# Where the tiles of a Trainium2 encoder kernel lie inside an SBUF partition

## The chip, the cores and the metric

The kernel runs on one core of one Trainium2 chip. The metric is the device time of one execution in microseconds (us), as the median over several runs. The kernel before takes 1402.52 us (three runs, 1402.32 to 1404.49).

## The reference, cut to what matters

One layer of a hybrid encoder block over a sequence of 256 positions with 2048 channels, all in float32. What is computed is almost wholly matrix products with large weights:

```
h = rms_norm(x, g_mix)
qa, ka, va, qb, kb, vb, qc, gates = split(h @ w_in)        # 2048 -> 4096 + 3 * 2048
oa, ob, oc = three attentions (mixer A dilated, B grouped-query, C over fixed memory tokens)
merged = sum over branches of sigmoid(gate_i) * (o_i @ w_br_i)
x = x + merged @ w_o                                        # 2048 -> 2048
hf = rms_norm(x, g_ffn) @ w_ffn_in                          # 2048 -> 2 * 5632
x = x + (silu(hf[:, :5632]) * hf[:, 5632:]) @ w_ffn_out     # 5632 -> 2048
```

## The kernel before

**Products.** The 256 positions are the output rows, in two tiles of 128. Weights come in blocks of 128 partitions by two times 512 columns of float32 (4096 bytes in each partition). Each block goes through three steps. SyncE's queue issues its load into a tile `raw` (line 202, `load`). ScalarE copies it, rounded, into a tile `whi`, and VectorE writes the remainder `raw - whi` into a tile `wlo` (lines 363 and 373, or 124 and 125): these are the two **halves** of a block. TensorE then makes three products of 128 by 128 by 512 for each piece: activations' high part with `whi`, high part with `wlo`, low part with `whi` (lines 225 to 227 in `product`, 402 to 404 in `pair`). The half of the weights is the moving operand, which streams 512 columns (2048 bytes of a partition) past the array; the activations (`memT`, `xT`, `oT`, `mT`, `x1T`, `hT` and the sums called `forms`) are the stationary operand, 128 columns (512 bytes) that a LDWEIGHTS brings in ahead of each matmul. In the profile a matmul is written as output<-moving,stationary, as in `mmZ<-whi,x1T`.

**Stages.** First the products of the memory tokens and of q, k and v, with the attentions beside them (`beginning`, then `product` at line 695); then four gate blocks and the branch A blocks (lines 701 to 709); then, in `everything()`, merging, the output projection, and the feed-forward layer. The stages of `everything()` use `pair`, which takes two blocks of weights at a time in a fixed order of steps (lines 53 to 58), some of them through a scheme of seven products in place of eight. `run` keeps TensorE four steps behind the halves (`run(everything(), 4)`, line 874). SyncE's queue and TensorE are held in the order of the program, and `follow` does the same for the halves on ScalarE and VectorE; the rest is placed by a scheduler.

**Pools.** All of these tiles lie in one SBUF partition's address range, at the same place in each of the 128 partitions. Pools are laid one behind another in the order in which they are opened, from low addresses up (`side="right"`: from the top down). Below them all lies a ring for DMA descriptors of 16,384 bytes. `wp` holds six `raw` tiles, four `whi` and four `wlo` of 4096 bytes each; `big` holds eleven tiles of 8192 bytes (`memT`, `xT`, `oT`, `x`, `x1T`, `mg`, most `forms`); `mid` five of 4096; `small` little ones. `early` (constants and loads of the start) and `s2` (sixteen tiles of 2048 bytes for heads of the attentions) are closed by `heads.close()` at line 711, and their room is given to two later pools: `tail` (four tiles of 8192 bytes: `mT`, `hT` and a few `forms`) and `more` (one further `whi` and one further `wlo`). `halves` (line 353) takes the tiles of `more` in every fifth call, and those of `wp` in the others:

```
356        pool, n = (more[0], 1) if more and count[0] % 5 == 0 else (wp, 4)
357        hi = pool.tile([P, PK, NC], F32R, name="whi", bufs=n)
358        lo = pool.tile([P, PK, NC], F32R, name="wlo", bufs=n)
```

Of the kernel before, what the change touches and what calls it, by code (L numbers as in the profile page):

```python
# [11 lines left out]
F32 = mybir.dt.float32  # L12
# [6 lines left out]
P = 128  # L19
# [6 lines left out]
NC = 512  # L26
KF = DFF // P
PK = 2
# [70 lines left out]
def encoder_block(ctx: ExitStack, tc: tile.TileContext, a: dict, out: bass.AP):  # L99
    nc = InOrder(tc)  # L100
    const = ctx.enter_context(tc.tile_pool(name="const", bufs=1))
    wp = ctx.enter_context(tc.tile_pool(name="wp", bufs=3))
    big = ctx.enter_context(tc.tile_pool(name="big", bufs=11))
    mid = ctx.enter_context(tc.tile_pool(name="mid", bufs=5))
    small = ctx.enter_context(tc.tile_pool(name="small", bufs=4))
    dram = ctx.enter_context(tc.tile_pool(name="dram", bufs=1, space=bass.MemoryType.DRAM))
    heads = ExitStack()
    early = heads.enter_context(tc.tile_pool(name="early", bufs=1))
    psum = ctx.enter_context(tc.tile_pool(name="psum", bufs=4, space=bass.MemoryType.PSUM))

    def s8(shape, name, dt=F32R, pool=None):
# [48 lines left out]
    side, now = [], [0]  # L160
# [33 lines left out]
    def finish():  # L194
        while side:
            tick()

    def load(src, k0, nk):

        raw = wp.tile([P, PK, NC], F32, name="raw", bufs=6)  # L200
        c = k0 % PK * NC
        nc.sync.dma_start(out=raw[:, :nk].rearrange("p k n -> p (k n)"), in_=src[k0 // PK][:, c:c + nk * NC])
        return raw

    def product(src, lhs, nk, head=(), beside={}):


        ps = [bank("mm", "mm") for _ in range(T)]
        k0 = 0
        while k0 < nk:  # L210
            n = head[0] if head else min(PK, nk - k0)
            head = head[1:]
            if k0 in beside:
                start(beside[k0])
            lhs(k0)
            raw = load(src, k0, n)
            hi = wp.tile([P, PK, NC], F32R, name="whi", bufs=4)
            lo = wp.tile([P, PK, NC], F32R, name="wlo", bufs=4)
            split(hi[:, :n], lo[:, :n], raw[:, :n])
            for i in range(n):  # L220
                k = k0 + i
                xh, xl = lhs(k)
                for t in range(T):
                    c = slice(t * P, (t + 1) * P)
                    nc.tensor.matmul(ps[t], lhsT=xh[:, c], rhs=hi[:, i], start=(k == 0), stop=False)
                    nc.tensor.matmul(ps[t], lhsT=xh[:, c], rhs=lo[:, i], start=False, stop=False)
                    nc.tensor.matmul(ps[t], lhsT=xl[:, c], rhs=hi[:, i], start=False, stop=(k == nk - 1))
                tick()
            k0 += n
        return ps  # L230
# [120 lines left out]
    count, more = [0], []  # L351
# [23 lines left out]
    def pair(src, lhs, order, done, forms=None, operand=None):  # L375
# [47 lines left out]
        def whole(u, c):  # L423
            def ready():
                if operand and c == 0:
                    operand(2 * u, True)
                raw = load((src(u, c),), 0, PK)
                if operand and c == 0:
                    if 2 * u + 2 < KT:
                        operand(2 * u + 2, True)  # L430
                    operand(2 * u)
                hi, lo = halves(raw)

                def products():
                    for k in range(2):
                        for t in range(T):
                            mul(("YV", "ZQ")[c][t], at(2 * u + k, t), hi[:, k], lo[:, k])
                return products
            return ready
# [3 lines left out]
        def first(u):  # L443
            def ready():
                b1, b2 = (load((src(u, c),), 0, PK) for c in range(2))
                held[u] = b1, b2
                hi, lo = halves(b1)

                def products():
                    mul("X", at(2 * u, 0), hi[:, 0], lo[:, 0])  # L450
                    mul("Y", at(2 * u + 1, 0), hi[:, 1], lo[:, 1])
                    if left["X"] == 2 * seven:
                        tl["A"], tl["B"] = s4([P, 2, NC], "SA"), s4([P, 2, NC], "SB")
                        copy(("A", 0), "X")
                return products
            return ready
# [252 lines left out]
            nc.vector.tensor_mul(mg[t][:, n0:n0 + NC], bp[t], sg[:, t])  # L709
    finish()  # L710
    heads.close()
    tail = ctx.enter_context(tc.tile_pool(name="tail", bufs=4))
    more.append(ctx.enter_context(tc.tile_pool(name="more", bufs=1)))
    mT, x1T, x = [], [], []
    ss1 = const.tile([P, T, 4], F32, name="ss1")

# [243 lines left out]
```

## Time and profile before

| | |
|---|---|
| median of three runs | 1402.52 us |
| profiled execution, its own time | 1403.52 us |
| its span | 1401.7 us, so 1.8 us lie around it |
| TensorE matmuls (PE) | 1384.8 us busy, 99% of the span, 6248 instructions |
| LDWEIGHTS (PEld) | 1137.0 us, 81% |
| VectorE (DVE) | 1118.3 us, 80% |
| ScalarE (ACT) | 807.7 us, 58% |
| granted TensorE clock, mean | 0.999 |
| HBM traffic | 197 GB/s over the span |

A busy PE in such a page is not a PE at its peak: matmuls overlap, and a matmul's recorded duration is longer than the distance to the next one's start. What a matmul costs in a full stream is the distance from start to start. The chain of waits shows that best: it merges successive matmuls of one output into pieces, each with its start, its length and the count (x3 is three matmuls).

### The profile page before, as it was taken

To read this page: it belongs to the slowest core of one execution; us is meant where nothing else is said; L and a number is where in the kernel's file an instruction comes from. 1 tells how busy PE (TensorE), PEld (TensorE's weight loads), DVE (VectorE), ACT (ScalarE), POOL (GpSimd) and SP (SyncE) were. 2 spreads that over 40 slices of the span, in tenths; PEclk is the share of its full clock that TensorE was granted. 3 is DMA by queue.
4 is the path that set the end of the run, shared out by engine and by line. 5 is a ranking of instruction groups with operands and counts; after the bars stand their busy time and mean duration, and the time that the engine had idled before them with its cause. 6 is when DMAs were issued, how large, how long until landed. Compare 5 with 4: busy or idle time off the path is not lost.

```text
span 1401.7 us, 17524 instructions
## 1 busy us (share of the span) xinstructions
PE 1384.8 (99%) x6248; PEld 1137.0 (81%) x6248; DVE 1118.3 (80%) x1474; ACT 807.7 (58%) x1093; POOL 76.7 (5%) x146
## 2 busy tenths in 40 slices
PE   8999999999999999999999999999999999999998
PEld 6778878888888888888888888888888888888887
DVE  5767756754798888788988997989988988988863
ACT  6766546544465564646665565655565665566632
POOL 0024533200000000000000000000000000000000
PEclk9999999999999999999999999999999999999999
DMA  8976535556565565755656665666655656565653
GB/s 300 336 238 212 164 103 189 161 161 192 173 232 201 182 213 179 272 177 182 195 168 207 210 184 192 195 210 195 214 189 183 222 179 203 191 198 191 222 167 125
DMA packets 79416, 277.09 MB, mean 198 GB/s; under 512 B 8992, under 2 KB 11552, under 8 KB 79072
## 3 DMA queue, kind: packets, MB, share of 16 engines
q1 hardware_dynamic: 79184, 275.94, 60.3%
q8 instruction: 49, 0.80, 0.2%
q14 instruction: 39, 0.32, 0.1%
q10 hardware_dynamic: 144, 0.02, 0.0%
HBM read 273.05 MB, written 2.88 MB: 197 GB/s over the span
## 4 chain that ended last, share of the span: by engine, by line
PE 92%; POOL 2%; DMA 2%; DVE 1%; ACT 1%; issue 1%; SPq 0%; DVEq 0%; ACTq 0%; POOLq 0%
PE mm L74 17%; PE mmZ L74 16%; PE mmV L74 16%; PE mmY L74 16%; PE mmQ L74 13%; PE mmX L74 9%; PE mmW L74 3%; DMA raw<-in_w_mem 2%; PE tp L74 1%; PE sc L74 1%; POOL rot L593 1%; DVE wlo L125 0%; POOL rot L590 0%; DMA rows<-in_mem 0%; PE o L74 0%
## 5 line engine op out<-in xcount | busy, mean ns | idle before, releaser
L363 ACT ACTIVATE whi<-raw 128x1024 fp32r<-128x1024 f32 (+1 forms) x454 | 451.5, 1004 | 343.2 <-PE mmQ L74 103.1
L373 DVE TENSOR_TENSOR wlo<-raw,whi 128x1024 fp32r<-128x1024 f32 (+1 forms) x454 | 517.9, 1154 | 106.9 <-ACT whi L363 104.6
L74 PE MATMUL mm<-whi,xT 128*128 128x512 f32 x768 | 244.0, 394 | 0.0
L125 DVE TENSOR_TENSOR wlo<-raw,whi 128x1024 fp32r<-128x1024 f32 x100 | 128.6, 1295 | 86.1 <-ACT whi L124 84.8
L74 PEld LDWEIGHTS mm<-whi,xT 128*128 128x128 f32 x768 | 144.0, 189 | 29.5 <-issue 0.8
L124 ACT ACTIVATE whi<-raw 128x1024 fp32r<-128x1024 f32 x100 | 105.6, 1070 | 89.9 <-PE mm L74 83.9
L74 PE MATMUL mm<-wlo,xT 128*128 128x512 f32 x384 | 150.8, 393 | 0.1
L74 PE MATMUL mmY<-whi,x1T 128*128 128x512 f32 x288 | 112.5, 392 | 0.0
L74 PE MATMUL mmV<-whi,x1T 128*128 128x512 f32 x288 | 109.7, 393 | 0.0
L373 DVE TENSOR_TENSOR wlo<-t,whi 128x1024 fp32r<-128x1024 f32 x74 | 72.5, 994 | 37.5 <-ACT whi L363 37.0
L363 ACT ACTIVATE whi<-t 128x1024 fp32r<-128x1024 f32 x74 | 63.0, 869 | 47.3 <-PE mmV L74 26.8
L74 PE MATMUL mmZ<-whi,x1T 128*128 128x512 f32 x224 | 87.5, 391 | 0.0
L74 PE MATMUL mmQ<-whi,x1T 128*128 128x512 f32 x224 | 87.4, 390 | 0.0
L74 PEld LDWEIGHTS mm<-wlo,xT 128*128 128x128 f32 x384 | 72.5, 189 | 15.7 <-issue 0.8
L74 PE MATMUL mmX<-whi,forms 128*128 128x512 f32 x232 | 78.9, 392 | 0.0
L74 PEld LDWEIGHTS mmY<-whi,x1T 128*128 128x128 f32 x288 | 54.0, 188 | 12.0
L74 PEld LDWEIGHTS mmV<-whi,x1T 128*128 128x128 f32 x288 | 54.0, 188 | 11.6
L74 PE MATMUL mmY<-whi,hT 128*128 128x512 f32 x156 | 60.6, 393 | 0.0
L74 PE MATMUL mmV<-whi,hT 128*128 128x512 f32 x156 | 60.2, 392 | 0.0
L74 PE MATMUL mmY<-wlo,x1T 128*128 128x512 f32 x144 | 56.3, 391 | 0.0
L74 PE MATMUL mmV<-wlo,x1T 128*128 128x512 f32 x144 | 56.3, 391 | 0.0
L74 PE MATMUL mmZ<-whi,hT 128*128 128x512 f32 x136 | 53.9, 396 | 0.0
(258 smaller groups left out, 2700.0 us busy)
## 6 DMA issues: line engine op xcount, KB each, us to landing
raw<-in_w_ffn SPq DMA_DIRECT2D x176, 512.0 KB, 4.3
raw<-in_w_gate SPq DMA_DIRECT2D x96, 512.0 KB, 4.2
raw<-in_w_ffn_out SPq DMA_DIRECT2D x88, 512.0 KB, 4.4
raw<-in_w_qkv SPq DMA_DIRECT2D x64, 512.0 KB, 4.5
raw<-in_w_o SPq DMA_DIRECT2D x32, 512.0 KB, 4.5
raw<-in_w_br SPq DMA_DIRECT2D x24, 512.0 KB, 4.3
raw<-in_w_mem SPq DMA_DIRECT2D x16, 512.0 KB, 5.7
rawT<-in_memT SPq DMA_DIRECT2D x8, 256.0 KB, 4.1
```

Source lines behind the costliest of these rows:

```text
L74: ins = op(*args, **kw)
L124: nc.scalar.activation(hi, src, AF.Copy)
L125: nc.vector.tensor_sub(lo, src, hi.bitcast(F32))
L363: nc.follow(nc.scalar.activation(hi[:, o], v, AF.Copy))
L373: nc.follow(nc.vector.tensor_sub(*due.pop(0)))
L593: op(ov[:, :, :, c], ov[:, :, :, c], tmp[:, :n])
```

## The change

Every instruction stays, and only the place of the tiles inside a partition is changed. `wp` now holds only the halves, behind `const` and `small` at the bottom of the partition, with a filler of 96 bytes (`fill`) that brings the first of them to byte 12288 = 3 x 4096. `raw` gets a pool of its own, `rp`, and `rp`, `big` and `mid` are laid from the top of the partition down. The ring for DMA descriptors shrinks to 8192 bytes. `more` is opened ahead of `tail`, so that it comes to lie right behind the four `wlo` of `wp`.

```
-    wp = ctx.enter_context(tc.tile_pool(name="wp", bufs=3))
-    big = ctx.enter_context(tc.tile_pool(name="big", bufs=11))
-    mid = ctx.enter_context(tc.tile_pool(name="mid", bufs=5))
     small = ctx.enter_context(tc.tile_pool(name="small", bufs=4))
+    wp = ctx.enter_context(tc.tile_pool(name="wp", bufs=4))
+    rp = ctx.enter_context(tc.tile_pool(name="rp", bufs=6, side="right"))
+    big = ctx.enter_context(tc.tile_pool(name="big", bufs=11, side="right"))
+    mid = ctx.enter_context(tc.tile_pool(name="mid", bufs=5, side="right"))
...
+    small.tile([P, 24], F32, name="fill", bufs=1)
...
-        raw = wp.tile([P, PK, NC], F32, name="raw", bufs=6)
+        raw = rp.tile([P, PK, NC], F32, name="raw")
...
     heads.close()
+    more.append(ctx.enter_context(tc.tile_pool(name="more", bufs=1)))
     tail = ctx.enter_context(tc.tile_pool(name="tail", bufs=4))
-    more.append(ctx.enter_context(tc.tile_pool(name="more", bufs=1)))
...
-    nc = _bacc.Bacc("TRN2", target_bir_lowering=False, num_devices=1)
+    nc = _bacc.Bacc("TRN2", target_bir_lowering=False, num_devices=1, dynamic_dma_scratch_size=8192)
```

The start addresses that the two built programs give to the tiles, in bytes from the start of a partition, with the remainder of a start by 128 (the same for all tiles of a row, since their sizes are multiples of 2048):

| tiles | before: first to last start | by 128 | after: first to last start | by 128 |
|---|---|---|---|---|
| `raw` (6) | 17,376 to 37,856 | 96 | 204,768 to 225,248 | 96 |
| `whi` of `wp` (4) | 41,952 to 54,240 | 96 | 12,288 to 24,576 | 0 |
| `wlo` of `wp` (4) | 58,336 to 70,624 | 96 | 28,672 to 40,960 | 0 |
| `whi`, `wlo` of `more` | 221,088 and 225,184 | 32 | 45,056 and 49,152 | 0 |
| `big` (11) | 74,720 to 156,640 | 96 | 114,656 to 196,576 | 96 |
| `mid` (5) | 164,832 to 181,216 | 96 | 94,176 to 110,560 | 96 |
| `s2` (16) | 196,512 to 227,232 | 32 | 53,248 to 83,968 | 0 |
| `tail` (4) | 188,320 to 212,896 | 32 | 53,248 to 77,824 | 0 |

On each of the five engines the built program has the same instructions in the same order as before, apart from the numbers of tiles. One wait moves. The tiles of `more` now lie where `gh`, `rope` and `rawT` of `early` lay, and those of `tail` no longer do, so the wait for the loads into `early` goes from one matmul to an earlier one. TensorE's list where the first matmul on a tile of `more` stands, as a difference between before (-) and after (+); `DMAHW` are semaphores of DMA queues, `PE`, `DVE` and `Activation` those of engines, and the words in brackets say what the matmul waits for:

```order
 L74 MATMUL mmV<-wlo,xT 128x512
 L74 MATMUL mmV<-whi,xT 128x512
-L74 MATMUL mmZ<-whi,xT 128x512 [waits PE_49,Activation_49]
+L74 MATMUL mmZ<-whi,xT 128x512 [waits DMAHW3_49,DMAHW5_49,DMAHW2_49,DMAHW6_49,DMAHW1_49,DMAHW7_49,DMAHW0_49,Activation_49]
 L74 MATMUL mmZ<-wlo,xT 128x512 [waits DVE_49]
 L74 MATMUL mmZ<-whi,xT 128x512
```

Thirty matmuls further on, the matmul that had the wait for the DMA semaphores is without it. Nothing else of the list has moved.

## The prediction

> **What bounds the kernel now.** The windows view comes first: busy time and number of instructions by engine, in four stretches cut where the chain changes character.
>
> ```profile
> core 0: us, PE busy (x) PEld busy (x) DVE busy (x) ACT busy (x) POOL busy (x), PEclk, DMA share, GB/s
> 0.00:54.50 54.50, 46.33 (x193) 37.07 (x194) 32.42 (x55) 35.64 (x56) 0.70 (x6) 1.00 0.82 304
> 54.50:383.73 329.23, 324.77 (x1556) 268.72 (x1554) 217.78 (x360) 184.77 (x332) 75.98 (x140) 0.99 0.59 187
> 383.73:1389.00 1005.27, 1005.08 (x4467) 824.45 (x4466) 864.97 (x1056) 587.29 (x707) 0.00 (x0) 1.00 0.61 197
> 1389.00:1401.70 12.70, 8.64 (x38) 6.75 (x36) 3.10 (x6) 0.00 (x0) 0.00 (x0) 1.00 0.24 83
> ```
>
> In the third stretch TensorE is never idle, at full clock, while VectorE has work for 86% of it (864.97 of 1005.27), ScalarE for 58% and the DMA engines for 61%. So there the time is the number of matmuls times the distance from one start to the next, and no other engine's wait ends last. This stretch holds 72% of the span. The second is nearly the same, with a few waits of the attentions; in the first the loads set the pace.
>
> So I ask next whether that distance is the same everywhere. The chain of waits gives it: start, length, what, and how many in a row. In the stretch of gates and branch A, where all halves come from `wp` and all stationary operands from `big`:
>
> ```profile
> 299.33 76.40 PE mm L74 x337
> ```
>
> That is 76.40 / 337 = 0.2267 us a matmul. In the merging stage I pick a step that takes its halves from `more` (worked out by counting the calls of `halves`), between two that don't. The stationary operand is `oT` or `xT`, from `big`, all through:
>
> ```profile
> 521.40 0.68 PE mmQ L74 x3
> 522.08 0.68 PE mmZ L74 x3
> 522.76 0.68 PE mmQ L74 x3
> ...
> 526.16 0.70 PE mmZ L74 x3
> 526.86 0.70 PE mmQ L74 x3
> 527.56 0.70 PE mmZ L74 x3
> 528.26 0.70 PE mmQ L74 x3
> 528.96 0.69 PE mmY L74 x3
> ```
>
> The four pieces from 526.16 are the twelve matmuls on `more`: 528.96 - 526.16 = 2.80 us, 0.2333 each, 6.6 ns more than the floor. Now the feed-forward's last product, with halves of `wp` and a stationary `hT`, from `tail`; then the same pairing right behind a step on `more`; then a step with both operands from the upper end, halves of `more` and a stationary `mT`:
>
> ```profile
> 1378.37 0.69 PE mmZ L74 x3
> ...
> 1385.24 0.69 PE mmZ L74 x3
> ...
> 902.74 0.70 PE mmZ L74 x3
> 903.44 0.70 PE mmQ L74 x3
> 904.14 0.70 PE mmZ L74 x3
> 904.84 0.70 PE mmQ L74 x3
> ...
> 635.67 0.68 PE mmQ L74 x3
> 636.35 0.68 PE mmZ L74 x3
> 637.03 0.68 PE mmQ L74 x3
> ```
>
> The first: (1385.24 - 1378.37) / 30 = 0.2290, 2.3 ns over the floor. The second: 0.2333, so this pairing has two paces, and which it takes depends on what ran before. The third: back at the floor, 0.2267. So neither `more` nor `tail` is slow in itself. What costs is that one operand of a matmul comes from the upper pools and the other from the lower ones. It isn't a longer load of the stationary operand either; by form and by tile, LDWEIGHTS takes the same from `big` and from `tail`:
>
> ```profile
> L74 PEld LDWEIGHTS mmV<-whi,x1T 128*128 128x128 f32 x288 | 54.0, 188 | 11.6
> L74 PEld LDWEIGHTS mmV<-whi,hT 128*128 128x128 f32 x152 | 28.6, 188 | 6.3
> ```
>
> Two things tell the upper pools from the lower in the table of addresses, and this trace can't part them. **Area**: they lie above some byte between 164,832 (the end of `big`) and 188,320 (the start of `tail`). **Remainder**: their starts leave 32 by 128, those of `wp` and `big` 96, so a mixed pair is 64 bytes apart in that count and an unmixed one 0.
>
> **How much there is to gain.** The third stretch's matmuls that aren't 512 wide are transposes, in the view of groups by form:
>
> ```profile
> L74 PE MATMUL tp<-ident,SA 128*128 128x128 f32 x88 | 13.2, 272 | 0.0
> L74 PE MATMUL tp<-ident,mg 128*128 128x128 f32 x32 | 4.8, 272 | 0.0
> L74 PE MATMUL tp<-ident,x 128*128 128x128 f32 x32 | 4.8, 272 | 0.0
> ```
>
> In the chain a group of four of them stands as one piece:
>
> ```profile
> 826.13 0.44 PE tp L74 x4
> ```
>
> These are 152, in 38 groups of four at 0.44 us: 16.7 us. The other 4467 - 152 = 4315 would take 978.2 us at the floor. 1005.27 - 978.2 - 16.7 leaves 10.3 us. The parts add up to about that: in the program's list 570 matmuls pair `more` with `big`, 570 x 6.6 ns = 3.8 us; 1059 pair `wp` with `tail`, between 1059 x 2.3 = 2.4 and 1059 x 6.6 = 7.0 us; together 6.1 to 10.8. Some of it will be the first matmuls after a group of transposes, so I take 9 us as what the mixed pairs cost.
>
> **The change, part by part.** *Order, waits, loads:* every engine's list is the same. The moved wait now stands ahead of the first matmul on `more`, with the whole of TensorE's queue behind it, and waits for loads of `early`. The last of those go out at 62.5 us and no load of `rawT` took over 11.9:
>
> ```profile
> L74 SPq DMA_DIRECT2D rawT<-in_xT x8: 328/328/505, 17.5 to 62.5; - x8
> DMA to landing us min/median/max: 2.5/5.1/11.9
> ```
>
> By 75 us they are in, and the matmul starts near 384: nothing. *`raw` at the top:* read by ScalarE and VectorE, written by DMA, never by TensorE. The rows hold no read of an upper `raw`. The nearest is VectorE's subtraction with `whi` and `wlo` in `more`: the 396 of its group, about a fifth of them in `more`, have one mean of 1222, so their place can't weigh much.
>
> ```profile
> L373 DVE TENSOR_TENSOR wlo<-raw,whi 128x1024 fp32r<-128x1024 f32 x396 | 480.7, 1222 | 102.5 <-ACT whi L363 100.8
> ```
>
> Should each take 5% more, that is 480.7 x 0.05 = 24 us on an engine with 140 us free in the third stretch: nothing on the path, and for the same reason there is room for TensorE to be faster. Below nothing there is no gain here either, as VectorE ends nothing. *`more` and `tail` moved down beside `wp`:* halves and `tail` now share both area and remainder (0). By area as by remainder these matmuls go to the floor: 570 of `more` with `big` and 1059 of `wp` with `tail`, the 9 us above, if nothing new is mixed. *The halves against `big`:* here the two readings part. All 4335 matmuls with a stationary operand of `big` now have a remainder of 0 against 96, 32 bytes apart, which no row of before shows. And the upper part of `big` now lies where `tail` lay: a quarter of `x1T` from 196,576, and `xT` from 172,000 and 180,192, which is in the gap that before tells nothing of.
>
> - By area: from 624 matmuls (edge at 188,000) to 1505 (edge at 172,032) are mixed. At 2.3 ns, the pace of the `hT` rows that no step on `more` goes ahead of, 1.4 to 3.5 us come back: net gain 5.5 to 7.6. At the dear pace the 1505 would take 9.9 us, and nothing would be left.
> - By remainder: 32 bytes apart costs nothing at one end (net gain 9), and as much as 64 bytes' dearer pace at the other (4335 x 6.6 ns = 28.6 us, net loss 20). Half of the cheap pace, 1.2 ns, would be 5 us and a net gain of 4. I take it to be near nothing: both cheap row and floor lie nearer to that than to the dear pace, which in the rows needs halves of `more` or a step on them just before.
>
> The Trainium skill bears on this: SBUF — State Buffer, "Who interferes with whom", says that TensorE has separate ports for the moving operand and for LDWEIGHTS, and that PE and ACT never wait on anyone. By that rule no placement would matter and the sum would be 0; the pieces of 0.70 beside those of 0.68 speak against it, at equal work and full clock.
>
> **Sum.** Profiled execution: 1403.52, of which 1401.7 is span. Gain by area 5.5 to 7.6, by remainder 4 to 9; I take 7, which lies in both. That gives 1396.5 for the profiled execution, and from the median of the runs (1402.52, 1 us below it) **1395.5 us**. What is late next is TensorE itself, at 0.2267 us a matmul.
>
> **The rivals.**
> 1. *The 32 bytes cost more than the old 64 (slower).* Place: every matmul on `big`, from the first stretch to the last. It decides from 9 us / 4335 = 2.1 ns a matmul; at the dear pace the net is +20: 1422. For it: mixed pairs cost in both directions, and 76% of the matmuls (4335 of 5,697) become a pair of this new sort. Against it: half the distance, and the floor is stable over every other address tried. 0.19.
> 2. *No change.* Either 32 bytes cost the cheap pace (4335 x 2.3 = 10 against 9), or the upper `big` eats the gain at the dear pace, or place has no part in it and the 0.70 come from something else that keeps step with `more`. All three leave 1402.5; 0.13 for the first two, 0.03 for the third, which the even rows at 526 us speak against. The Trainium skill's rule on ports, above, is the third. In all 0.16.
> 3. *Much faster.* The halves start at a remainder of 0 for the first time. If the floor itself holds a step like the 6.6 ns seen between placements, the 5,697 matmuls of that width in the program's list lose 38 us more: 1402.5 - 9 - 38 = 1355. For it: all rows of before, floor included, start 32 bytes off a multiple of 64. Against it: no quoted piece is below the floor. 0.13. The Trainium skill's TensorE: Matmul & The Clock Gate, "Wait — 56ns, not 53.3ns?", gives 215.7 ns from start to start for 512 columns, 11 ns under the floor here; by that page up to 5,697 x 11 = 63 us could be had, as an estimate, and no run here shows it.
>
> **How the numbers follow.** My forecast (4 to 9 us faster, 1393 to 1399) gets 0.52. About 0.2% (2.8 us) is what a measurement of this kernel can tell from no change. Faster: 0.52 + 0.13 = 0.65; same 0.16; slower 0.19. The range is to hold 0.8: forecast, no change, and rival 1 up to its full price of 1422, which leaves the much faster case out: 1385 to 1422, the lower end a margin for a floor that falls by 1 to 2 ns.
>
> **What would show it.** Right: pieces on `more` and on `tail` of 0.68 for three in the chain, as the ones from 635.67 have now; the long piece of `mm` still near 0.2267 a matmul; some pieces on a quarter of `x1T` at 0.69. Rival 1: the long `mm` piece longer than 76.40 for the same count. Rival 3: shorter. Wrong altogether: pieces on `tail` still at 0.69 or 0.70 though halves and `tail` agree in both area and remainder, or a TensorE that waits in the third stretch.

## The result and the profile after

After: **1418.66 us**, the median of four runs (1418.5 to 1419.42). Before on the same chip: 1402.42 (four runs, 1401.75 to 1404.49). The ratio is 1.0114, with a 95% interval of 1.0097 to 1.0132: slower by 16 us, where 1395.5 was forecast, inside the range and close to rival 1.

The windows view of the kernel after, cut at the same places of the program to within some ten matmuls (columns as before):

```profile
core 0 of [0], span 1417.6 us
0.00:54.50 54.50, 47.83 (x193) 38.02 (x194) 33.00 (x57) 36.55 (x57) 0.70 (x6) 1.00 0.85 308
54.50:386.50 332.00, 328.30 (x1543) 266.36 (x1542) 215.27 (x352) 183.80 (x330) 75.28 (x140) 0.99 0.58 184
386.50:1405.00 1018.50, 1018.27 (x4479) 825.67 (x4478) 867.26 (x1061) 591.23 (x708) 0.00 (x0) 1.00 0.60 195
1405.00:1417.60 12.60, 8.54 (x38) 6.75 (x36) 3.09 (x6) 0.00 (x0) 0.00 (x0) 1.00 0.24 83
```

TensorE still never waits in the third stretch, the clock is full, VectorE and ScalarE do the same work and the DMA engines move the same bytes. So the 16 us are not a wait. The matmuls themselves stand further apart, and the chain of waits says which. First the long piece of gates and branch A, then the first pieces of merging, all with halves of `wp` and a stationary operand of `big`:

```profile
302.31 78.64 PE mm L74 x337
380.94 0.70 PE mmY L74 x3
381.64 0.70 PE mmV L74 x3
382.34 0.70 PE mmY L74 x3
383.04 0.70 PE mmV L74 x3
383.74 0.70 PE mmZ L74 x3
```

The long piece has grown from 76.40 to 78.64 for the same 337, from 0.2267 to 0.2334 us each; this is the sign that the prediction named for rival 1. The first pieces of merging were, in before:

```profile
375.73 0.68 PE mmY L74 x3
376.41 0.68 PE mmV L74 x3
```

They stood at 0.68 and stand at 0.70. Now the feed-forward's last product, halves of `wp` with `hT` of `tail`, whose pieces in before took 0.69:

```profile
1390.42 0.68 PE mmZ L74 x3
...
1397.22 0.68 PE mmY L74 x3
```

(1397.22 - 1390.42) / 30 = 0.2267. These are at the floor, as forecast. So one half of the change brought what it was to bring, and the other half cost more. The load of the stationary operand took no longer for that, nor did VectorE's subtraction from an upper `raw` (by form; columns: count, busy us, mean ns, idle before):

```profile
L74 PEld LDWEIGHTS mmV<-whi,x1T 128*128 128x128 f32 x288 | 54.0, 188 | 12.9
L376 DVE TENSOR_TENSOR wlo<-raw,whi 128x1024 fp32r<-128x1024 f32 x396 | 480.8, 1223 | 107.7 <-ACT whi L366 106.5
```

188 and 1223 ns, where before had 188 and 1222.

### The profile page after: what moved, and what is told of

Its sections match the earlier page's. It is cut to its first block, busy times and chain, and to the rows that moved or that the text cites. A ratio compares the mean times of both kernels' runs of the same rounds, so it can differ in the third digit from the quotient of the medians.

```text
span 1417.6 us, 17523 instructions
## 1 busy us (share of the span) xinstructions
PE 1402.9 (99%) x6248; PEld 1136.8 (80%) x6248; DVE 1118.6 (79%) x1474; ACT 811.6 (57%) x1093; POOL 76.0 (5%) x146
## 4 chain that ended last, share of the span: by engine, by line
PE 95%; POOL 2%; DVE 1%; issue 0%; ACT 0%; DMA 0%; DVEq 0%; SPq 0%; POOLq 0%
PE mm L74 17%; PE mmZ L74 17%; PE mmV L74 17%; PE mmY L74 16%; PE mmQ L74 14%; PE mmX L74 9%; PE mmW L74 3%; PE tp L74 1%; POOL rot L596 1%; PE sc L74 1%; PE o L74 1%; POOL rot L593 0%; PE pT L74 0%; PE hT L74 0%; POOL rtmp L594 0%
## 5 line engine op out<-in xcount | busy, mean ns | idle before, releaser
L74 PE MATMUL mm<-whi,xT 128*128 128x512 f32 x768 | 247.8, 399 | 0.0
```

Source lines behind the costliest of these rows:

```text
L74: ins = op(*args, **kw)
```

## The experiments

**Theory.** What counts is the difference between the start of the moving operand (the halves) and that of the stationary operand, taken by some power of two. "Difference" below always means moving minus stationary. **Rivals:** *area* (upper addresses of a partition are slow); *A*, something else in the change slows the matmuls on `big`: `raw` at the top, the smaller ring, the new place of `big`; *S*, each operand's own start has to be round, whatever the other's. Under the theory it stays open by what number the difference counts, whether the sign matters, and what each difference costs.

Every kernel leaves the computation whole; only places change. Ratios are to before, run beside it on the same chip (medians there 1403.33, 1403.35 and 1404.31 in the three sets).

**1. Only `tail` and `more` moved, in the kernel before.** 64 bytes more in `small`, which lies below `early`, `s2`, `tail` and `more`, bring `tail` and `more` to 2016 by 2048, where `wp` and `big` are at 992 (1024 bytes apart, which is 0 by 128 and by 512):

```
     early = heads.enter_context(tc.tile_pool(name="early", bufs=1))
+    small.tile([P, 16], F32, name="fill", bufs=1)
```

> The kernel before with 64 bytes more ahead of its upper pools, so that tail and more leave 96 by 128, as wp and big do; nothing else moves. R128 and R512: the 10 us of the third stretch go but for what follows transposes, about 1393 us. Theory area (upper part of the partition against lower): no change, 1402.4.

Measured 1394.46 us, ratio 0.9940 (0.9927 to 0.9952), span 1392.6: 9 us faster than before. The same two places of its chain, the long piece and the step of merging that takes its halves from `more` (mmZ, mmQ, mmZ, mmQ; in before it began at 526.16, at 0.70 a piece), with the piece behind it:

```profile
299.08 76.41 PE mm L74 x337
...
524.41 0.68 PE mmZ L74 x3
525.09 0.68 PE mmQ L74 x3
525.77 0.68 PE mmZ L74 x3
526.45 0.68 PE mmQ L74 x3
527.13 0.68 PE mmY L74 x3
```

A move of 64 bytes, with the pools in the same area, takes away all that the mixed pairs cost. Area falls. The 9 us that the prediction worked out for them were right.

**2. `big`, `mid` and `raw` moved by multiples of 32 bytes, in the kernel after.** A tile of 96, 32 or 64 bytes at the very top moves all that hangs from there down; the halves stay at 0. Of the first:

```
+    top = ctx.enter_context(tc.tile_pool(name="top", bufs=1, side="right"))
+    top.tile([P, 24], F32, name="top")
     rp = ctx.enter_context(tc.tile_pool(name="rp", bufs=6, side="right"))
```

With 24 elements, so that `big` agrees with the halves by 128 (difference +128):

> The changed kernel with a filler of 96 bytes at the top, so that raw, big and mid start at a remainder of 0 by 128, as the halves do; by 512 they still differ by 128. Theory R128 (what costs is the difference of the starts of a matmul's moving and stationary operand by 128, and the 4335 matmuls on big are slowed by 32 bytes): all matmuls at 0.2267 us, 1418.7 - 28 = about 1391 us, the long mm piece 76.4 us for 337. Rival A (the place of raw at the top, the small descriptor ring, or the area of big costs): stays within 1415 to 1419. Rival R512 (the difference counts by 512 or more): 128 bytes apart still cost, 1400 or over.

Measured 1417.79 us, ratio 1.0104 (1.0090 to 1.0118). The long piece:

```profile
302.63 78.32 PE mm L74 x337
```

No cure. The remainder by 128, in which the prediction counted, is not the one that matters, or rival A is right. With 8 elements (difference +64), and with 16 (+96):

> The changed kernel with 32 bytes at the top: big starts 64 by 128, the halves 0, so the stationary operand starts 64 under the moving one, as wp with tail did before. R128: those pairs ran at 0.2290 or at 0.2333 us before, so 4335 matmuls cost 10 to 29 us over big_by_128: 1401 to 1420. Rival A: 1415 to 1419 as after.

> The changed kernel with 64 bytes at the top: big starts 32 by 128, the halves 0, the mirror image of the change's -32. R128 with both directions alike: as after, 1416 to 1420. If the direction counts: between 1391 and 1416. Rival A: 1415 to 1419.

Measured 1401.95 us, ratio 0.9991 (0.9982 to 1.0000), and 1420.94 us, ratio 1.0129 (1.0113 to 1.0144). The long piece of the first, then of the second:

```profile
300.78 77.13 PE mm L74 x337
```

```profile
301.52 78.63 PE mm L74 x337
```

+64 costs (77.13 - 76.40) / 337 = 2.2 ns a matmul, the cheap pace that `wp` with `tail` had in before, also +64 apart. +96 costs 6.6 ns, as +32 does. The price doesn't grow with the distance. And rival A is weakened: `raw` and the ring hardly differ between these kernels, and the time moves by 19 us.

**3. The halves moved instead.** The filler of `small` is cut from 96 to 64 bytes, and `big`, `raw` and the ring stay as in after. Halves, `tail` and `more` then start at 2016 by 2048, as `big` does (difference 0):

```
-    small.tile([P, 24], F32, name="fill", bufs=1)
+    small.tile([P, 16], F32, name="fill", bufs=1)
```

> The kernel after with the filler in `small` cut from 96 to 64 bytes: halves, `tail` and `more` all start 32 bytes lower, at 2016 by 2048, where `big` and `raw` stand unmoved; so every matmul has both operands at the same remainder. Raw tiles stay at the top, the ring stays at 8192. Theory (only the difference between the starts of the moving and of the stationary operand counts): all 4335 pairs on `big` go back to 0.2267, long piece of `mm` 76.4 for 337, time 1392 to 1396, like before_tail_64. Rival A (something else of the change slows matmuls on `big`: raw at the top, the ring, the place of `big` itself): 1415 to 1420. Rival S (the halves have to start at a multiple of 128 or more, whatever the other operand): also 1415 or more, and the pieces on `tail` at 0.69 or 0.70.

Measured 1394.52 us, ratio 0.9939 (0.9927 to 0.9952). Its long piece, and the same step on `more` in merging:

```profile
299.50 76.41 PE mm L74 x337
...
524.84 0.68 PE mmZ L74 x3
525.52 0.68 PE mmQ L74 x3
526.20 0.68 PE mmZ L74 x3
526.88 0.68 PE mmQ L74 x3
527.56 0.68 PE mmY L74 x3
```

32 bytes are the whole loss: 1418.66 against 1394.52. With everything else of the change in place the time is that of experiment 1, so A falls, and so does S, since no start here is rounder than 32 bytes. The moved wait, `raw` at the top, the ring and the order of the pools are worth nothing that shows.

Without any filler (the line taken out) the halves are 96 bytes lower, and the difference is -64:

> The kernel after without the filler: halves, `tail` and `more` 96 bytes lower, 416 by 512, `big` unmoved at 480; the pairs on `big` are -64 apart, the difference that `more` with `big` had in before (0.2333), opposite in sign to that of before's `wp` with `tail` and of big_less_64 (0.229). If the sign counts: long piece about 78.6 for 337 and 4335 x 6.6 = 28.6 us over the floor of 1394: 1418 to 1424. If only the distance counts: as big_less_64, long piece 77.1, 1400 to 1404. If -64 is dear only where a step on other pairs goes before: near 1402 too.

Measured 1420.67 us, ratio 1.0126 (1.0112 to 1.0140):

```profile
302.70 78.63 PE mm L74 x337
```

The sign counts: +64 costs 2.2 ns, -64 costs 6.6. This also prices the filler in the change as made. It brought at most some 2 us (1420.67 to 1418.66, in different sets, and the intervals of the two ratios overlap); 32 bytes less of it would have brought 26.

**4. By which number the difference counts.** The tile at the top with 56 elements (224 bytes, difference +256), and with 120 (480 bytes, difference +512):

> The kernel after with 224 bytes at the very top: `raw`, `big` and `mid` 224 bytes lower, at 256 by 512 and 0 by 256; halves at 0 by 4096. Difference 256. If the difference counts by 256: every pair at the floor, 1392 to 1396, long piece 76.4. If it counts by 512 or more, 256 is one more distance with a price of its own, as 128 had (5.7 ns): 1405 to 1420.

> The kernel after with 480 bytes at the very top: `raw`, `big` and `mid` 480 bytes lower, at 0 by 512 and 1536 by 2048; halves at 0 by 4096. The stationary blocks inside a tile are 512 bytes apart, so a difference of 512 can't well cost something of its own. If the difference counts by 512 or less: every pair at the floor, 1392 to 1396, long piece 76.4. If it counts by 1024: 1400 to 1422. Rival A (raw at the top or the ring): 1415 to 1420. Rival 3 of the prediction (halves and `big` both at a round start lower the floor itself): long piece under 76.0.

Measured 1393.74 us, ratio 0.9932 (0.9918 to 0.9945), and 1393.87, ratio 0.9935 (0.9922 to 0.9947). The long piece of the first; then, of the second, the long piece:

```profile
298.52 76.41 PE mm L74 x337
```

```profile
298.56 76.41 PE mm L74 x337
```

Both are at the floor: 256 bytes apart is as good as 0, and 128 is not. So of the powers of two it is 256, and the reading by 512 or more falls. Rival 3 falls too: in the second kernel halves and `big` all start at 0 by 512, and the floor is the same 0.2267.

**5. The two differences still missing, -32 and +160.** The filler of `small` with 8 elements; the tile at the top with 32.

> The kernel after with the filler in `small` cut from 96 to 32 bytes: halves, `tail` and `more` 64 bytes lower, 448 by 512, `big` unmoved at 480: difference -32, which is 224 by 256. Theory (signed difference by 256): a price of its own between nothing and 6.6 ns, so 1394 to 1423, no forecast within that. If only the distance counted it would be the price of +32: long piece 78.6, 1417 to 1421.

> The kernel after with 128 bytes at the very top: `raw`, `big` and `mid` 128 bytes lower, 352 by 512, halves at 0: difference +160, which by 256 is -96. Theory (signed difference by 256): between nothing and 6.6 ns, so 1394 to 1423. If only the distance by 256 counted, it would be the price of +96: long piece 78.6, 1418 to 1423.

Measured 1418.98 us, ratio 1.0101 (1.0086 to 1.0116), and 1422.96, ratio 1.0134 (1.0117 to 1.0150):

```profile
301.14 78.63 PE mm L74 x337
```

```profile
302.39 78.94 PE mm L74 x337
```

The price of -32 is that of +32, and +160, which is -96, costs 7.5 ns where +96 costs 6.6. Put together, with the long piece divided by 337:

| difference by 256 | kernel (label of its run) | long piece, us | ns a matmul | time, us |
|---|---|---|---|---|
| 0 | five kernels, before among them | 76.40 to 76.41 | 226.7 | 1393.7 to 1394.5 (without before) |
| 32 | after | 78.64 | 233.4 | 1418.7 |
| 64 | big_less_64 | 77.13 | 228.9 | 1402.0 |
| 96 | big_plus_32 | 78.63 | 233.3 | 1420.9 |
| 128 | big_by_128 | 78.32 | 232.4 | 1417.8 |
| 160 | big_160 | 78.94 | 234.2 | 1423.0 |
| 192 | halves_less_96 | 78.63 | 233.3 | 1420.7 |
| 224 | halves_less_64 | 78.63 | 233.3 | 1419.0 |

Before has 0 for `wp` with `big`, but +64 for `wp` with `tail` and -64 for `more` with `big`. In the kernel after, `wp` with `tail` is at 0 and everything with `big` at 32.

That the difference alone sets the price is shown at two values. At 0 the floor came with both starts at 224, at 160 or at 0 by 256. At +64 the cheap pace came with 224 and 160 in before and with 0 and 192 in big_less_64. Each of the other prices was measured at one pair of starts (-64 twice, at the same pair), so for those it is not shown that other starts with the same difference would cost the same.

All four kernels in which every pair is at 0 by 256 (experiments 1, 3 and 4) beat both the kernel before and the change. The lowest, 1393.74, is 0.68% under before; the differences among the four are within their intervals.

## Why the prediction was wrong

*What bounds the kernel:* right. TensorE's distance from start to start sets the third stretch in every run, and no wait took its place in any: between 400 and 1370 us TensorE is busy for 969.8 of the 970 us in each of the twelve kernels.

*That mixed pairs cost, and 9 us in all:* right. Four kernels with no mixed pair are 8.8 to 9.6 us under before by the medians. Why +64 had two paces in before, 0.2290 and 0.2333, is not settled: in big_less_64, where no pair at -64 goes ahead, the long piece and the pieces of merging at +64 show only the cheap one, which fits the prediction's remark that it hangs on what ran before.

*Area or remainder:* the prediction kept both readings open. Experiment 1 decides against area, and experiment 4 for a remainder by 256.

**The step that failed** is the sentence on the new pairs, "I take it to be near nothing", said of the 32 bytes between the halves and `big`. What was put near 0 us measured 24.1 (1418.66 against 1394.52 in experiment 3), against the 9 that the rest of the change was to bring. It had two grounds. One was that the price grows with the distance, the same thought as in the first words against rival 1, "half the distance". The runs show no such growth: +32 costs three times what +64 does. The other was that the dear pace "needs halves of `more` or a step on them just before". The long piece of after is dear, 0.2334, with halves of `wp` alone, and it stands ahead of the first matmul on `more`. Nor did 128 hold as the number to count by. The trace of before held a hint: 0.2290 for `wp` with `tail` and 0.2333 for `more` with `big`, which the prediction counted as one distance of 64 bytes. They are +64 and -64, and experiments 2 and 3 show that these have two prices.

*Rival 1's mechanism and its size:* the mechanism is what happened; 1422 at full price, measured 1418.66. The count of 4335 was a little short: by the names of the tiles, after's records hold 193, 1224 and 2987 matmuls on `big` in the first three stretches, 4404 in all. Against experiment 3 the loss is 24.1 us, or 24.1 / 4404 = 5.5 ns a matmul, not 6.6. The windows show where the rest went. The kernel at +512, cut alike:

```profile
54.50:383.00 328.50, 324.19 (x1552) 268.42 (x1551) 217.01 (x358) 184.05 (x331) 75.82 (x140) 0.99 0.58 186
383.00:1379.30 996.30, 996.07 (x4466) 824.84 (x4465) 864.04 (x1056) 586.56 (x707) 0.00 (x0) 1.00 0.61 199
```

In the third stretch a TensorE instruction takes 996.30 / 4466 = 223.1 ns here and 1018.50 / 4479 = 227.4 in after: 4.3 ns more, over 4479 of them 19.3 us. The 2987 matmuls on `big` among them are the ones 32 apart, so 6.5 ns each, the full price. In the second stretch it is 328.50 / 1552 = 211.7 against 332.00 / 1543 = 215.2, 3.5 ns over 1543, so 5.4 us for the 1224 matmuls on `big`, 4.4 ns each. Two pieces of that stretch, of after and then of the kernel at +512:

```profile
54.47 22.86 PE mm L74 x98
...
225.29 14.45 PE mm L74 x62
```

```profile
53.77 22.54 PE mm L74 x98
...
222.79 14.07 PE mm L74 x62
```

The 62 are (14.45 - 14.07) / 62 = 6.1 ns further apart each, nearly the full price. The 98 are only 3.3 ns further apart, since at +512 they already take 0.2300 each. Around such pieces TensorE waits for the attentions (328.30 busy of 332.00), and in the first stretch the loads set the pace. That waits which were there before take up the rest of the price is argued from these rows; no run was made for it.

*The rival of no change, and the rule on ports:* the Trainium skill's SBUF — State Buffer, "Who interferes with whom", by which PE never waits on anyone, was weighed in the prediction as a reason for no change. The measurement decides against reading it so: with the same instructions in the same order the place of two operands, both read by TensorE, moves the time from 1393.7 to 1423.0 us.

*The terms put at nothing* (the moved wait, `raw` at the top): right, by experiment 3, which keeps both and reaches 1394.52.

*Rival 3:* ruled out for these starts by experiment 4; no run got below 0.2267 us.

## What to carry to other kernels

In a kernel whose TensorE never waits, look at the distance from start to start, piece by piece, before looking for waits: pieces of 0.70 beside pieces of 0.68 were worth 9 us in before and 24 in after. Then print the start addresses of both matmul operands, and pad so that their difference is 0 by 256. At that difference it made no difference here how round each start is by itself. This was shown for 512 columns of float32 with a stationary operand loaded ahead of each matmul; elsewhere it is to be tried. When a trace shows a price at one offset, don't interpolate to another: an untried offset is unknown, and a pad of a few bytes tries it.

## What had not been expected of the hardware

The price of an offset neither grows with it nor is it the same in both directions: 6.6, 2.2, 6.6, 5.7, 7.5, 6.6, 6.6 ns a matmul of 512 columns at +32 to +224 by 256, in steps of 32, and nothing at 0, +256, +512 and 1024 (the last in experiment 1). The recorded LDWEIGHTS of `mmV<-whi,x1T` takes 188 or 189 ns in every run. Whether the price is paid because the reads of the two operands get in each other's way is not shown: no run here takes the two reads apart. Starts that aren't multiples of 32 bytes, and matmuls of other widths, were not tried.
